# The first recurrence's columns taken out of the mixer, by seven products for eight, and the recurrence run beside the delta rule

## The chip, the core and the metric

The kernel runs on one core of a Trainium2 chip. The metric is device time in microseconds, the median of several runs. The engines are TensorE (PE; its weight loads are PEld), VectorE (DVE), ScalarE (ACT), GpSimd (POOL) and SyncE (SP), which here only starts DMAs.

## The reference, cut to what matters

One layer of a decoder: a feed-forward block (FFN), a mixer, a second FFN, a final norm, on 512 tokens of 1024 channels in float32.

```
h = x + 1/2 * SwiGLU_1(RMSNorm(x))
h = h + HybridMixer(RMSNorm(h))
h = h + 1/2 * SwiGLU_2(RMSNorm(h))
y = RMSNorm_final(h)
...
proj = (u @ w_in)
(hq, hf, hi, hg, gq, gk, gv, ga, gb, gz, gate_h, gate_g) = split(proj)
```

The mixer has two branches. The first recurrence (HGRN2, 8 heads) uses hq, hf, hi, hg: a forget gate from hf, a query silu(hq), values hi, an output gate silu(hg); its state is carried over chunks, its output normed and gated. The second (gated delta rule, 16 value heads, 8 query/key heads) uses gq, gk, gv after a short causal convolution, decays from ga and gb, an output gate silu(gz), and in each chunk the inverse of a unit lower triangular matrix. Each branch is projected to 1024 channels, the two are merged by sigmoid(gate_h) and sigmoid(gate_g), and one more projection follows.

## The kernel before, in words

Every operand of a large product is split into a high and a low half (`fp32r`), and three products (high by high, low by high, high by low; `mm3`, lines 188 to 191) stand for one float32 product. A "column" is 128 output channels for all 512 tokens: 8 slices of the 1024 input channels, three products each, so 24 products of 512 columns. Weights are read as `raw` tiles of 128 x 512; ScalarE casts the high half, VectorE subtracts for the low half. In some units the low half is made otherwise: ScalarE writes the negated high half, and a DMA started by GpSimd adds the weight from memory to it ("fold", lines 329 to 334).

**The FFNs** (`ffn`, line 448) run as a `stream` (line 282): a list of units, each one weight tile with its products. Before unit t runs, its halves must be there; `ahead` prepares up to some eight units in advance, in two lanes of three buffers. `posts` are what is done behind a unit, `hooks` what is done ahead of it. The first three pairs of columns (in the second FFN) are plain, 48 products of 512 columns a pair, while the norm is measured (`stats`, line 230) and the normalised operands are made (`operands`, line 426). The others are made by `fast` (line 354): a pair of columns as a two by two block product in Winograd's form, seven products for eight, 7 x 4 x 3 = 84 products of 256 columns, with sums of weights (`comb`) and of results (`sums`, lines 380 to 387) on VectorE.

**The mixer** (line 688) is ordered by a planner, `Desk` (line 64): each piece of work is a generator that asks for engines with estimated costs, buffers and events; the planner takes at each step the piece of lowest rank that is ready on an engine, and what it emits is the order of the instructions. SyncE's transfers are planned so too. `DENSE` (line 34) lists the columns in order: F and Q are hf and hq, B is hi and hg in natural layout (tokens on the partitions), D the decays, k, q, v, z the delta rule's, y the first branch's projection; the 16 gate columns t are taken when nothing else may start. `choose` (line 1679) says what each needs, `loader` (line 1696) starts the weight loads, `maker` (line 1728) splits them, `product` (line 1762) issues the products. The mixer's operands `uh`, `ul` are the input times its gain, but not times the norm: `norm` (line 1828) finds the norm, and each result is multiplied by it afterwards, on VectorE (`rbc`, in `h_q`, `h_f`, `conv`, `tgate`, `zgate`) or by a scalar (`rcol`, `h_v`, `gate`).

`h_head` (line 902) is one head of the first recurrence: products `pd` of queries and keys (line 917, four of 192 columns, in plain float32, two records each in the trace), seven levels of masked products `pl` (lines 974 and 980), mask copies (`copy_predicated`, line 938, four for each of the levels 2 to 16), then the chunks. Its eight heads stand, in `DENSE`, beside F, Q, B; most of the delta rule (`g_e`, `g_n`, `g_b`, `g_w`, `g_inv`, `g_rec`) comes behind them, when their buffers are passed on (`claim`, `more`). The triangular inverse of the delta rule runs on GpSimd. The heads' outputs stay in SBUF, split, as operands of y. `operand` (line 1526) reads the delta heads' outputs back for the last projection.

FFN and mixer each stand in a `tc.manual_schedule` block: inside of one, each engine's instructions keep the order in which they are written.

## Time and profile before

| | |
|---|---|
| median of three runs | 1606.91 us (1606.55 to 1606.93) |
| profiled execution, span | 1604.7 us |
| mean granted TensorE clock | 0.997 |
| instructions | 29242 |
| DMA | 204.91 MB, mean 128 GB/s |

The span reaches from the first to the last instruction of one profiled execution; the median of the runs is 2.2 us longer, with what lies around it. In the profile's rows a group stands by line, engine, operation and tiles, with its count, its busy time (overlaps counted once) and the mean duration of one, then the idle time ahead of it and what ended that. A duration of a product is longer than its place in the pipeline: products overlap. The table by stretches gives for each engine the busy time and, in brackets, the instructions. In the row of DMA issues the last number is the median time from issue to landing.

By time: the first FFN runs to about 358 us, the mixer to about 1245, the second FFN to the end; the masked products of the first recurrence run from 393 to 604, the delta rule to about 1110, the last two projections the rest.

### The profile page before, as it was taken

The numbers are of one execution on the slowest core, as the hardware profiler recorded it, in microseconds if no ns is written. First come the engines' busy times: TensorE is split into PE (matmuls) and PEld (weight loads), VectorE is DVE, ScalarE is ACT, GpSimd is POOL, SyncE is SP. The second block draws the span as 40 slices with busy tenths as digits, with TensorE's granted clock in tenths as the row PEclk, the third lists the DMA queues.
The fourth block names the chain that finished last, engine by engine and source line by source line (L and its number), as shares of the span: only waits on it lengthen the run. The fifth ranks groups of instructions, "written<-read, shape, count | busy, mean of one in ns | idle before, by whom it ended". The sixth has DMA issues, their size and how long they took to land.

```text
span 1604.7 us, 29242 instructions
## 1 busy us (share of the span) xinstructions
PE 1593.7 (99%) x10672; PEld 1386.3 (86%) x10672; DVE 1145.7 (71%) x2259; ACT 831.0 (52%) x1872; POOL 408.8 (25%) x725
## 2 busy tenths in 40 slices
PE   9999999999999999999999999999999999999997
PEld 8999998888888888888888888888888899999887
DVE  6888785447787778668788888765545788878433
ACT  5766674332434345456665665554324666667222
POOL 0211212001221221156545556600001121121001
PEclk9999999999999999999999999999999999999998
DMA  5766863332312322443242334445543586686333
GB/s 187 168 162 156 181 160 103 113 117 86 106 47 68 86 92 87 137 135 104 93 125 80 119 107 129 134 136 186 164 142 128 140 183 158 154 187 146 92 91 117
DMA packets 121824, 204.91 MB, mean 128 GB/s; under 512 B 21184, under 2 KB 27072, under 8 KB 121680
## 3 DMA queue, kind: packets, MB, share of 16 engines
q1 hardware_dynamic: 104688, 172.40, 34.3%
q0 software_dynamic: 14400, 26.22, 10.2%
q10 hardware_dynamic: 2592, 4.42, 1.0%
q8 instruction: 84, 1.38, 0.4%
q14 instruction: 60, 0.49, 0.1%
HBM read 188.02 MB, written 14.97 MB: 126 GB/s over the span
## 4 chain that ended last, share of the span: by engine, by line
PE 91%; DMA 3%; issue 3%; DVE 2%; ACT 0%; POOL 0%; POOLq 0%; SPq 0%; DVEq 0%; ACTq 0%
PE pmm L189 19%; PE pmm L191 19%; PE pmm L190 19%; PE px L191 6%; PE px L190 6%; PE px L189 6%; DMA wlo<-w1a 2%; PE pnat L189 2%; PE pnat L191 2%; PE pnat L190 2%; PE pgq L1189 1%; PE pw L1387 1%; PE pog L1403 1%; PE pl L974 1%; PE pd L917 1%
## 5 line engine op out<-in xcount | busy, mean ns | idle before, releaser
L189 PE MATMUL pmm<-uh,whi 128*128 128x512 f32 x879 | 361.3, 411 | 0.0
L191 PE MATMUL pmm<-uh,wlo 128*128 128x512 f32 x879 | 343.0, 390 | 0.0
L190 PE MATMUL pmm<-ul,whi 128*128 128x512 f32 x879 | 341.9, 389 | 0.0
L191 PE MATMUL px<-xs,wlo 128*128 128x256 f32 x1008 | 285.7, 283 | 1.3 <-DMA wlo<-w1a 0.7
L190 PE MATMUL px<-xs,whi 128*128 128x256 f32 x1008 | 285.2, 283 | 0.0
L189 PE MATMUL px<-xs,whi 128*128 128x256 f32 x1008 | 285.2, 283 | 0.0
L1754 ACT CAST whi<-raw 128x512 fp32r<-128x512 f32 x226 | 140.2, 621 | 242.7 <-PE pmm L190 195.2
L1756 DVE TENSOR_TENSOR wlo<-raw,whi 128x512 fp32r<-128x512 f32 x226 | 158.3, 702 | 118.2 <-ACT whi L1754 116.2
L191 PEld LDWEIGHTS pmm<-uh,wlo 128*128 128x128 f32 x879 | 165.0, 188 | 36.1 <-DVE wlo L607 0.2
L191 PEld LDWEIGHTS px<-xs,wlo 128*128 128x128 f32 x1008 | 193.5, 192 | 2.1 <-DMA wlo<-w1a 1.1
L189 PEld LDWEIGHTS px<-xs,whi 128*128 128x128 f32 x1008 | 193.5, 192 | 0.1
L190 PEld LDWEIGHTS px<-xs,whi 128*128 128x128 f32 x1008 | 193.5, 192 | 0.1
L189 PEld LDWEIGHTS pmm<-uh,whi 128*128 128x128 f32 x879 | 165.5, 188 | 30.4
L190 PEld LDWEIGHTS pmm<-ul,whi 128*128 128x128 f32 x879 | 165.7, 189 | 29.5 <-DVE ul L216 0.2
L329 ACT CAST whi<-sw 128x512 fp32r<-128x512 f32 x144 | 87.6, 613 | 92.8 <-DVE sw L366 72.6
L308 DVE TENSOR_TENSOR wlo<-raw,whi 128x512 fp32r<-128x512 f32 x100 | 77.7, 788 | 76.7 <-ACT whi L329 76.3
L329 ACT CAST whi<-raw 128x512 fp32r<-128x512 f32 x104 | 61.2, 592 | 125.6 <-PE pmm L190 92.8
L227 POOL TENSOR_TENSOR acc<-acc,sqt 128x512 f32<-128x512 f32 x18 | 23.4, 1302 | 319.8 <-ACT sqt L225 319.8
L308 DVE TENSOR_TENSOR wlo<-sw,whi 128x512 fp32r<-128x512 f32 x144 | 98.0, 681 | 0.0
L329 ACT CAST whi<-rw 128x512 fp32r<-128x512 f32 (+1 forms) x130 | 79.6, 613 | 26.6 <-PE px L190 13.4
L190 PE MATMUL pmm<-xs,whi 128*128 128x512 f32 (+1 forms) x238 | 89.7, 377 | 0.1
L189 PE MATMUL pmm<-xs,whi 128*128 128x512 f32 (+1 forms) x238 | 89.8, 377 | 0.0
(476 smaller groups left out, 3223.5 us busy)
## 6 DMA issues: line engine op xcount, KB each, us to landing
raw<-wt SPq DMA_DIRECT2D x160, 256.0 KB
rw<-w1b SPq DMA_DIRECT2D x80, 256.0 KB
rw<-w1a SPq DMA_DIRECT2D x74, 256.0 KB
wlo<-w1b POOLq DMA_DIRECT2D x53, 256.0 KB, 4.8
wlo<-w1a POOLq DMA_DIRECT2D x47, 256.0 KB, 5.0
raw<-w2b SPq DMA_DIRECT2D x41, 256.0 KB
raw<-w2a SPq DMA_DIRECT2D x36, 256.0 KB
raw<-wn SPq DMA_DIRECT2D x32, 256.0 KB
```

What stands on the lines that cost most here:

```text
L189: pe.matmul(pt, ah, bh, start=first, stop=False)
L190: pe.matmul(pt, ah, bl, start=False, stop=False)
L191: pe.matmul(pt, al, bh, start=False, stop=last)
L227: add.tensor_tensor(acc, acc, s, op=ALU.add)
L308: dve.tensor_tensor(lo, x, hi.bitcast(F32), op=ALU.subtract)
L329: act.copy(hi, x)
L917: pe.matmul(pd[c // 2][:, (c % 2) * 192:(c % 2) * 192 + 192], ke[:, c * P:(c + 1) * P], qq[:, c], start=True, stop=True)
L974: pe.matmul(pl_[s0:s0 + 32, c * 16:(c + 1) * 16], ke[:, c * P + s0:c * P + s0 + 32], qv[:, c, r, :, 1], start=True, stop=True)
L1189: pe.matmul(pq[:, (c % 2) * 256:(c % 2) * 256 + 256], kq[:, c, 0], kq[:, c].rearrange("p a b -> p (a b)"), start=True, stop=True)
L1387: pe.matmul(pw[:, hd2[i]], ut[:, 4 * i + c], xs[i], start=True, stop=True)
L1754: act.copy(hi, raw)
L1756: dve.tensor_tensor(lo, raw, hi.bitcast(F32), op=ALU.subtract)
```

## The change

A new stage, `projections`, stands between the first FFN and the mixer, in a `manual_schedule` block of its own, with two streams one behind the other.

- The first (pool `fp`): the eight columns of F and Q each, in pairs. Three pairs are plain (24 products of 512 columns a column) while the norm is measured; five go through `fast`, generalised by `outs`. Results go to memory (`qd`, `fd`), normed, Q through silu. `operands` gets a late form that leaves the normalised input, split, in `uh`, `ul`; four DMAs of GpSimd move half of it there. `decays`, before a piece of the planner's work, is done here at fixed units.
- The second (pool `bp`, opened after `fp` closes): `natural`, twice, each half of the columns of values and gates in natural layout as a block product with seven products for eight: 28 units of two times three products of 512 columns. The first product's four units and the third's four are folded. Results go to memory (`vd`, `gd`, silu on the gates). The first column of k follows in the same stream; its result is handed to the mixer in PSUM.

The stream's end now also runs posts that lie behind the last unit. In the mixer the columns F, Q, B, D are gone from `DENSE`, k0 too; the delta rule's come first, y last. Nothing is multiplied by the norm any more: `conv` and `tgate` read PSUM through ScalarE, `zgate` through ScalarE and VectorE. The heads read Q, F, values and gates back (`h_q`, `h_f`, `h_v`; Q into runs of 32 floats) and run at rank 2.5; each pair uses eight buffers `op`, reused. `pd` is made by sixteen products of 32 rows and 48 columns a head, and the masks up to 16 work on a compact tile `ac`, one copy a level in place of four, spread by four copies of ScalarE at the end. The heads' outputs go to memory (`hod`); `h_out` reads them back into `uh`, `ul` when all columns but y are done ("inputs"). Buffers of the delta rule are handed on by `give`, `allot`, `back`, `retire`. The gates' results all go through memory.

```diff
 DENSE = (
-    "F0 Q0 F1 Q1 B0 F2 Q2 F3 Q3 B1 D0 F4 Q4 F5 Q5 B2 F6 Q6 F7 Q7 B3 "
-    "k0 q0 k1 q1 y0 y1 y2 y3 v0 v1 y4 y5 y6 y7 k2 q2 v2 v3 z0 z1 k3 q3 v4 v5 z2 z3 k4 q4 v6 v7 z4 z5 "
-    "k5 q5 v8 v9 z6 z7 k6 q6 v10 v11 z8 z9 k7 q7 v12 v13 z10 z11 v14 v15 z12 z13 z14 z15 "
+    "q0 v0 v1 k1 q1 z0 z1 v2 v3 k2 q2 z2 z3 v4 v5 k3 q3 z4 z5 v6 v7 k4 "
+    "q4 z6 z7 v8 v9 k5 q5 z8 z9 v10 v11 k6 q6 z10 z11 v12 v13 k7 q7 z12 z13 v14 v15 z14 z15 "
+    "y0 y1 y2 y3 y4 y5 y6 y7 "
...
+RINGS = {False: RB, True: RW, "near": 8, "far": 5}
+AHEAD = tuple((k, i) for i in range(8) for k in "FQ")
+SLOW = 3
+HR = 2.5
...
+        for t in sorted(t for t in posts if t >= len(units)):
+            for f in posts[t]:
+                f()
...
+    def natural(p, xo, bp, at, posts):
...
+        units = []
+        for i in range(4):
+            units.append(Unit([a11[i], a21[i]], raw(a11[i]), prod(0, i, "mm"), drop=(a11[i],), fold=a11[i].src))
+        for i in range(4):
+            units.append(Unit([a22[i]], of("s2", i), prod(2, i, "aa"), comb=lambda i=i: sums(i)))
+        for i in range(4):
+            units.append(Unit([a12[i]], raw(a12[i]), prod(3, i, "bb"), drop=(a12[i],), fold=a12[i].src,
+                              comb=lambda i=i: comb("s4", i, a12[i], "s2", ALU.subtract)))
+        for n, o, lanes in (("s1", 1, "de"), ("s3", 4, "mm"), ("s4", 5, "aa")):
+            units += [Unit([], of(n, i), prod(o, i, lanes)) for i in range(4)]
+        for i in range(4):
+            units.append(Unit([], raw(a22[i]), prod(6, i, "bb"), drop=(a22[i],)))
+        return units
+
+    def projections(c0, ahead, weights, to, follow):
+
+        with tc.tile_pool(name="xp", bufs=1) as xp, \
+                tc.manual_schedule(engines={x.engine for x in (pe, act, dve, pool, sp)}):
+            xs = xp.tile([P, 24, T], F32R, name="xs")
...
+            with tc.tile_pool(name="fp", bufs=1) as fp:
...
+                for i in range(2 * SLOW):
+                    x, held = plain(weights(ahead[i]), KD, ux, lane if i < 2 else mm, fold=i > 3, roomy=lambda k: i % 2)
+                    units += x
...
+                    def two(v, i=i, o=o):
+                        act.activation(o[0][:, second], v["uc"][:, second], **shape(ahead[i]))
+                        sp.dma_start(to(ahead[i]), o[0])
+
+                    def three(v, i=i, o=o):
+                        act.activation(o[1][:, first], v["uc"][:, first], **shape(ahead[i + 1]))
+                        act.activation(o[1][:, second], v["vb"], **shape(ahead[i + 1]))
+                        sp.dma_start(to(ahead[i + 1]), o[1])
+                    units += fast([weights(x) for x in ahead[i:i + 2]], xo, fp, len(units), posts, (one, two, three), False)
...
+                stream(units, fp, 3, hooks, posts)
+            with tc.tile_pool(name="bp", bufs=1) as bp:
+                units, posts = [], {}
+                for p in range(2):
+                    units += natural(p, xo, bp, len(units), posts)
+                x, held = plain(weights(follow), KD, ux, lane, roomy=lambda k: "near")
+                units += x
+                stream(units, bp, 3, {}, posts)
+            return held["pt"]
...
-        for c in range(NT):
-            pe.matmul(pd[c // 2][:, (c % 2) * 192:(c % 2) * 192 + 192], ke[:, c * P:(c + 1) * P], qq[:, c],
-                      start=True, stop=True)
+        for c in range(NT):
+            for r in range(4):
+                s0 = 32 * r
+                pe.matmul(pd[s0:s0 + 32, c * 48:(c + 1) * 48], ke[:, c * P + s0:c * P + s0 + 32], qq[:, 4 * c + r],
+                          start=True, stop=True)
...
+    def h_out(k):
+
+        yield "on", ("oh", k), "inputs"
+        yield "get", "ta", 1
+        yield S
+        og = ta("og")
+        sp.dma_start(og, hod[k])
+        yield "lag", LAG["back"]
+        yield *A(512), 1
+        act.copy(uh[:, k], og)
+        yield *V(512), 1
+        dve.tensor_tensor(ul[:, k], og, uh[:, k].bitcast(F32), op=ALU.subtract)
...
     def conv(k, i, pt, out, n, lane="mm"):
-        dve.tensor_tensor(ci[:, 3:], pt, rbc, op=ALU.mult)
+        act.copy(ci[:, 3:], pt)
...
+    D.start((3, 8, -1), conv(("k", 0), 8, e["opened"], lambda: st[0]["kq"][:, :, 0], NT, "a"))
     D.start((3, -1), loader())
     D.start((9,), product())
     for i in range(8):
-        D.start((2, i), h_head(i))
+        D.start((HR, i), h_q(i))
+        D.start((HR, i), h_f(i))
+        D.start((HR, i), h_head(i))
+        D.start((7, i), h_out(i))
     for i in range(4):
-        D.start((2, i), h_pair(i))
+        D.start((HR, i), h_v(i))
```

More of the change, by code (lines that the diff above doesn't have):

```diff
@@ L509, in ffn, with silu, close @@
             for p in range(slow, KF):
-                units += fast(w1, p, xo, fp, len(units), posts, gate)
+                first, second = slice(0, 256), slice(256, 512)
+                def silu(n):
+                    return lambda v: act.activation(v[n][:, second], v[n][:, second], AF.Silu)
+                def close(v, p=p):
+                    gate(p, (v["ua"][:, second], v["uc"][:, second]), (v["uc"][:, first], v["vb"]))
+                units += fast([w1[ORDER[p], n] for n in range(2)], xo, fp, len(units), posts,
+                              (silu("ua"), silu("uc"), close), p >= 15 or p < 7)
             end = len(units)
@@ new lines, in give, with allot, back @@
+    def give(name, *items):
+        for x in items:
+            if (name, 7) in D.at:
+                retire(name, x)
+            else:
+                free[name].append(x)
+                D.put("p" + name)
+    def allot(name):
+        for u in range(8):
+            yield "get", "p" + name, 1
+            st[u][name] = free[name].pop(0)
+            D.fire((name, u))
+        for x in free[name]:
+            retire(name, x)
+    def back(u, *names):
+        for n in names:
+            give(n, st[u][n])
@@ L1117, in g_e @@
     def g_e(u, st):
[L1119 to L1120 removed]
+        yield "on", ("at", u), *([("E", u - 1)] if u else [])
         for i in range(2):
@@ L1658, in more @@
-        pool.memset(G["ut2"], 0.0)
-        D.fire(("ut", 2))
+        pool.memset(ut, 0.0)
+        new("ut", ut)
         e_ = ex(7, P, 4, 256)
-        for i, n in enumerate(("x", "we", "w")):
-            G[n].append(e_[:, i])
-        G["tp"].append(e_[:, 3].rearrange("p (a b) -> p a b", a=8))
-        D.fire("more")
+        new("rw", tuple(e_[:, i] for i in range(3)))
     todo = [(w[0], int(w[1:])) for w in DENSE.split()]
-    gates = [("t", i) for i in range(16)]
+    gates = [("t", i) for i in range(16) if i not in ahead]
@@ L1693, in choose @@
                 return x
-        return gates.pop(0) if len(gates) > (KEEP if todo else 0) else None
+        return gates.pop(0) if len(gates) > (KEEP if any(x[0] != "y" for x in todo) else 0) else None
     def loader():
```

913 lines of the change are left out of this document (422 added, 491 removed).

## The prediction

> **What bounds the kernel now.** The page comes first: busy times, then the slices, then the chain.
>
> ```profile
> span 1604.7 us, 29242 instructions
> PE 1593.7 (99%) x10672; PEld 1386.3 (86%) x10672; DVE 1145.7 (71%) x2259; ACT 831.0 (52%) x1872; POOL 408.8 (25%) x725
> PE   9999999999999999999999999999999999999997
> PEclk9999999999999999999999999999999999999998
> PE 91%; DMA 3%; issue 3%; DVE 2%; ACT 0%; POOL 0%; POOLq 0%; SPq 0%; DVEq 0%; ACTq 0%
> ```
>
> TensorE is busy in 1593.7 of 1604.7 us, in every slice but the last, at the full granted clock, and 91% of the chain that ended last is TensorE. So a microsecond of products removed is a microsecond gained, and a microsecond in which TensorE finds nothing ready, anywhere, is one lost. The change has to be added up in these two kinds.
>
> The table by stretches gives the price of a product where products run without a break, and the load of the other engines.
>
> ```profile
> core 0: us, PE busy (x) PEld busy (x) DVE busy (x) ACT busy (x) POOL busy (x), PEclk, DMA share, GB/s
> 1364.00:1404.10 40.10, 40.10 (x336) 40.10 (x336) 33.79 (x61) 25.05 (x50) 7.76 (x9) 1.00 0.68 154
> 1484.30:1524.50 40.20, 40.20 (x179) 33.28 (x178) 16.29 (x23) 10.99 (x20) 2.59 (x2) 1.00 0.32 92
> 361.00:682.00 321.00, 321.00 (x2674) 265.69 (x2673) 245.75 (x608) 133.91 (x324) 66.17 (x93) 1.00 0.30 89
> 682.00:1083.00 401.00, 401.00 (x2626) 332.77 (x2625) 319.90 (x701) 245.59 (x714) 213.79 (x490) 1.00 0.37 116
> 842.50:882.60 40.10, 40.10 (x283) 33.30 (x282) 35.67 (x84) 23.72 (x76) 22.66 (x55) 1.00 0.25 80
> ```
>
> First row, the seven-for-eight stage of the second FFN: 336 products of 256 columns in 40.10 us, 0.1193 us each. Second row, its plain products of 512 columns: 40.20 / 179 = 0.2246 us. The third row is roughly the first recurrence, the fourth the delta rule: VectorE is at 77% and 80%, and at 89% in the fullest stretch (last row) with TensorE still never idle.
>
> **The change, part by part: what goes.** Sixteen columns of F and Q are 16 x 24 = 384 products of 512 columns, 86.2 us. After: six plain columns (144 products, 32.3 us) and five pairs by seven products (5 x 84 = 420 of 256 columns, 50.1 us), 82.4 in all: **-3.8**. The values and gates in natural layout are
>
> ```profile
> L189 PE MATMUL pnat<-whi,uh 128*128 128x512 f32 x72 | 29.9, 415 | 0.0
> L189 PE MATMUL pnat<-wx,uh 128*128 128x512 f32 x56 | 22.6, 404 | 0.0
> L917 PE MATMUL pd<-qq,ke 128*128 128x192 f32 x64 | 11.5, 326 | 0.0
> L980 PE MATMUL pl<-qp,ke 128*32 128x32 f32 x128 | 2.8, 197 | 0.0
> L974 PE MATMUL pl<-qp,ke 128*32 128x16 f32 x1024 | 11.8, 185 | 0.0
> ```
>
> 128 products of each of three kinds, 384, 86.2 us; after, 2 x 7 x 4 x 2 x 3 = 336, 75.5 us: **-10.8**. The first score of each head (pd) now costs 64 records, 11.5 us; it becomes sixteen products of 32 rows and 48 columns a head, 256 records. Bounds: at the 11.5 ns of the 16-column products (11.8 / 1024) 2.9 us, at 1.5 times the 22 ns of the 32-column ones (2.8 / 128) 8.4. The second is nearer in shape: **-3**, ends -8.6 and 0. The Trainium skill (TensorE: Matmul & The Clock Gate, "Wait — 56ns, not 53.3ns?") states that starts of matmuls never follow each other closer than about 25 ns; by it the 256 take 6.4 us and this term is an estimated -5. The trace disagrees with that floor: 11.5 ns each in the last row.
>
> What remains of TensorE's work (delta rule, levels, transposes, all other columns) keeps its count, and interruptions of long products by short ones move with the short ones. Sum of what goes: **-17.6**.
>
> **What comes: the seam between the two new streams.** The FFN's weights reach the mixer early, since one hand-ordered block's instructions may overtake another's:
>
> ```profile
> 353.30 0.93 SPq L1712 DMA_DIRECT2D raw<-wt  x2
> 356.90 0.33 SPq L558 DMA_DIRECT2D hd<-h  x1
> 1244.13 0.69 DVE L1901 SCALAR_TENSOR_TENSOR h<-pmm,hr 128x512 f32<-128x512 f32 x1 [1.48 <-PE pmm L191]
> 1244.90 0.80 SPq L301 DMA_DIRECT2D rw<-w1b  x2
> 1247.68 0.62 ACT L329 CAST whi<-rw 128x512 fp32r<-128x512 f32 x1 [1.57 <-DMA rw<-w1b]
> ```
>
> The mixer's weight load at 353.30 goes ahead of the FFN's last spill at 356.90. But the second FFN's first load into a buffer of its own pool waits for the mixer's last instruction (1244.13 + 0.69) and starts at 1244.90; its data is used at 1247.68, 2.8 us later. In the change, both new streams stand in one block, so nothing overtakes, and the second's buffers lie where the first's were. The second's first four units also have their low half made by an accumulating DMA. So TensorE waits through a chain, from rows of the FFN:
>
> ```profile
> L385 DVE TENSOR_TENSOR uc<-px,uu 128x512 f32<-128x512 f32 x16 | 10.9, 681 | 0.0
> L407 ACT ACTIVATE uc<-uc 128x256 f32<-128x256 f32 x16 | 6.7, 418 | 4.8 <-DVE uc L385 4.8
> L329 ACT CAST whi<-rw 128x512 fp32r<-128x512 f32 x49 | 30.4, 620 | 7.9 <-PE px L190 6.4 <-DMA rw<-w1b 1.5
> L333 ACT ACTIVATE wlo<-whi 128x512 fp32r<-128x512 f32 x41 | 25.9, 632 | 1.3
> wlo<-w1b POOLq DMA_DIRECT2D x53, 256.0 KB, 4.8
> L588 PE MATMUL pwarm<-ones 128*128 128x128 f32 x22 | 4.8, 415 | 1.1 <-DVE mhalf L165 1.1
> L243 PE MATMUL pbc<-sq,rcol 128*128 128x128 f32 x16 | 2.1, 275 | 0.0
> ```
>
> Last sum 0.7; three activations 1.3; the store of the last column, which stands ahead of the loads on SyncE and holds the pool, 0.3 + 2.8 (no row has a store's landing; the load's is taken); the third load, 0.9 after the first, 2.8; cast and negation for two units (the second is prepared first) 2.5; accumulating DMA 4.8. With 0.5 for hand-overs, 16.6. Then the clock: the page's last slice shows it falling after short idle, and at the start 22 records of 128 columns take 4.8 us where 16 take 2.1 (2.9 for 22) later: 1.9 lost on each restart. **+18.5**; without the wait for the store and one unit's casts 14, with the twelve queued loads slowing the accumulation (4.8 doubled) 23.
>
> **The seam into the mixer.** SyncE's order in the mixer puts its rank first: the heads' Q, F, values and gates (six transfers, 2 MB; rank 2.5) ahead of the weights (rank 3). They go to the new pool, which waits for the old one's last store: sums 1.4, activation 0.7, store 3.1, then six issues of 0.4 and a load of 2.8, 10.4 after the last natural product; if 2 MB pass first at the 154 GB/s of the FFN row above, 13 us instead of 2.4, so 21. I take 13; cast and low half 1.3; less the one plain column kept to cover this, 24 x 0.2246 = 5.4; with 1.9 for the clock, **+11**, ends 0 (nothing held) and 19. The Trainium skill (DMA: Bandwidth & Descriptors, "Specifications") states that transfers under 512 B fall to read-modify-write; Q goes in by runs of 128 B, so by it the estimate would lean to the upper end. No row here shows it.
>
> **Smaller terms.** The y columns now wait until every other column is done, since their operands take the place of the normalised input:
>
> ```profile
> L1541 ACT CAST uh<-og 128x512 fp32r<-128x512 f32 x5 | 3.0, 617 | 0.0
> L1543 DVE TENSOR_TENSOR ul<-og,uh 128x512 fp32r<-128x512 f32 x5 | 3.3, 684 | 0.0
> ```
>
> At least 0.6 + 0.7 after the last such product, with the load 4.5, in an order laid out for later data 8: **+3**. In the fast stage VectorE carries the FFN's 33.79 of 40.10 and some 9 us of decays and operands over 50 us, near its fill: **+1** (0 to 5). In the mixer it loses the multiplications by the norm, three quarters of the mask copies and 64 weight halves, and does the rest, below 565.7 us (245.75 + 319.90), beside some 540 of products: about 81% by my count, under the 89% above; scalar work rises, hidden under its 61%: **+2** (0 to 10).
>
> At nothing I cost the added transfers: F, Q, values and gates go out by 32 stores of 256 KB and come back by 24 loads, the heads' outputs out and back by 16, some 21 MB in all. They lie beside products on queues that the rows above show 30% to 37% busy; if that cover were gone, 21 MB at the 116 GB/s of the fourth row would be 180 us, so even a tenth of it unhidden would outweigh everything else, and the six of them ahead of the mixer's first weights are that tenth's likeliest place, priced above. Behind a held load on SyncE stand all later loads and stores of its block, and TensorE waits for the first of them; elsewhere six prepared weight halves of buffer (three pairs a lane) cover it. The decays, moved into the fast stage, keep their products, and their table changes and VectorE work stand in that stage's +1.
>
> Sum: -17.6 + 18.5 + 11 + 3 + 1 + 2 = +17.9. 1604.7 + 17.9 = 1622.6; the median of the runs lies 2.2 above the span, so **1625**. With every term at its low end (-23.2 + 14 + 0 + 1.3) it would be 1599, with every term at its high end (-14.6 + 23 + 19 + 8 + 5 + 10) 1657; the ends do not fall together, and the forecast's own range is 1609 to 1643.
>
> **Rivals.**
> - *Seams covered.* If SyncE and ScalarE prepare the next stream while TensorE is still on the old one, as at 353.30, both seams cost nothing and the sum is -17.6 + 3 + 2: 1594 (1587 to 1600), faster. It decides where a stream's first weights are ready before the old stream's last product. For: no seam in the trace shows idle. Against: those are seams between blocks, and their first loads need no new pool.
> - *One seam.* If only the first one stalls, or the second does with half the first, the sum is near 0 to +7: 1605 to 1613.
> - *The end of the delta rule uncovered.* The gate columns, now used up as fill, no longer stand behind its last heads; eight y columns (43 us) do. If its last chain lags more than that, TensorE waits, perhaps 20 us on top: 1645. Against: the fourth row's POOL at 53% leaves slack.
> - *Not what it says*: if the recurrence still runs mostly ahead of the delta rule, only placement differs and no term changes.
>
> **Chances.** Forecast 0.56, covered 0.27, one seam 0.11, uncovered end 0.06. Only covered is clearly faster, and the one-seam case splits over all three. A measurement tells 0.2%, about 3 us, from no change. Faster 0.29, same 0.06, slower 0.65. The range takes in most of the covered case and of the forecast: 1590 to 1643; the forecast's own is 1609 to 1643.
>
> **What would show it.** Of after: idle of TensorE of over 10 us ahead of the first natural products, ended by an accumulating DMA; a second gap at the mixer's first columns, ended by a weight half; granted clock under 1.00 in both slices; 336 products of natural layout; pd with 256 records. If these gaps are absent, my reading of the order is wrong and the covered case holds; if pd or the fast stage costs more, the removal was mis-sized; idle among the last heads speaks for the uncovered end.

## The result, and the profile after

The changed kernel takes 1672.93 us (median of 4 runs, 1670.91 to 1674.61) where the kernel before takes 1606.92 (1606.55 to 1607.59): 1.0414 times as long, 95% interval 1.0401 to 1.0427. Forecast were 1625 us and a range of 1590 to 1643. The sign was the forecast one; the loss, 66 us, is more than three times the 18 that the sum gave.

The page of the profile after, to be read beside that of before: span, busy times, TensorE and its granted clock by slices, and the chain.

```profile
span 1671.7 us, 30224 instructions
...
PE 1603.4 (96%) x10996; PEld 1389.5 (83%) x10996; DVE 1145.7 (69%) x2168; ACT 910.8 (54%) x2025; POOL 433.6 (26%) x761
...
PE   9999999999959799999999999999999999999997
...
PEclk9999999999979999999999999999999999999999
...
PE 78%; DMA 8%; issue 7%; DVE 3%; ACT 1%; POOL 1%; SPq 0%; POOLq 0%; ACTq 0%; DVEq 0%
```

Two of forty slices fall to 5 and 7; elsewhere the tenths are too coarse to show anything. In the chain TensorE fell from 91% to 78%, and DMA and issue rose from 3% each to 8% and 7%. VectorE is busy for the same 1145.7 us as before.

The table by stretches of the changed kernel (columns as in the prediction: busy time and count of PE, PEld, DVE, ACT and POOL, granted clock, DMA share, GB/s) finds the places. The stretches are: the end of the plain F and Q columns, the fast stage, the seam between the streams, a stretch across the seam's end, the natural stage with its column k0, and the seam into the mixer.

```profile
362.00:395.00 33.00, 29.30 (x126) 24.03 (x125) 21.80 (x30) 16.69 (x26) 6.33 (x7) 0.95 0.59 166
395.00:460.90 65.90, 61.11 (x462) 58.76 (x460) 50.31 (x81) 46.47 (x83) 10.99 (x13) 0.95 0.65 168
460.90:480.00 19.10, 0.80 (x1) 0.29 (x1) 5.12 (x8) 6.86 (x13) 3.48 (x4) 0.62 0.81 235
465.60:486.10 20.50, 6.83 (x15) 5.07 (x16) 10.37 (x17) 7.14 (x12) 3.48 (x4) 0.50 0.98 286
480.00:575.30 95.30, 88.10 (x359) 70.04 (x359) 61.72 (x100) 46.41 (x78) 11.80 (x17) 0.95 0.53 141
575.30:586.30 11.00, 1.32 (x5) 0.71 (x4) 4.27 (x11) 2.94 (x6) 1.79 (x3) 0.64 1.01 285
```

None of these stretches has the full clock, not even those that the prediction thought covered. The view of TensorE's waits (total, times, longest, in us) gives each its cause; of the kernel before, the same view from 361 to 1244 us is empty.

```profile
PE pxn L197 <- DMA wlo<-wn: 14.6, 6, 7.4
PE pxn L196 <- ACT whi L336: 10.9, 1, 10.9
PE ptk L1284 <- DVE h L1255: 5.6, 1, 5.6
PE pmm L196 <- ACT whi L1841: 4.1, 1, 4.1
PE pbc L250 <- POOL rcol L259: 3.7, 1, 3.7
PE pn L593 <- issue: 3.5, 1, 3.5
PE pmm L196 <- ACT uh L1595: 3.0, 2, 1.5
PE pks L1508 <- DVE sm L1314: 2.1, 1, 2.1
```

The first row has six waits: 7.4 us end the first seam, five more, 7.2 us together, lie inside the natural stage. Rows 3 and 4 are the seam into the mixer, rows 5 and 6 the norm's spread and the decays' transposes, row 7 the last heads of the delta rule.

**The account.** Each product is given the start-to-start interval that its like has in an undisturbed stretch (226 ns for 512 columns, 120 for 256, 151 and 15 for the two forms of pd, and so on); the sum is TensorE's work. Of what the intervals are longer, those over 0.9 us are counted as waits, those in periods of half granted clock as half clock, and the rest as small delays. From the end of the first FFN to the start of the second:

```
                            total   work   waits  half clock  small
before  361 to 1244         883.0  838.8     0.0      0.0     44.2
after   362 to  395          33.1   27.2     3.9      1.6      0.3
        395 to  460.5        65.5   57.0     4.9      2.5      1.1
        460.5 to 480         19.5    0.3    19.1      0.0      0.0
        480 to  575          95.0   80.9     8.0      4.5      1.7
        575 to  586.4        11.8    0.9    10.2      0.8      0.0
        586.4 to 1311       724.2  652.2    14.6     10.2     47.2
after, sum                  949.1  818.5    60.6     19.6     50.4
after less before           +66.1  -20.3   +60.6    +19.6     +6.2
```

The work fell by 20.3 us, as it should; 60.6 us of waits and 19.6 of half clock came in its place. Some 35 us of it lie at the two seams (29.3 of waits, 6 of half clock), the rest in stages that the prediction took to be covered or nearly so.

### The profile page after: what moved, and what is told of

Same layout as the page of the kernel before. It is cut to its first block, busy times and chain, and to the rows that moved or that the text cites. A ratio compares the mean times of both kernels' runs of the same rounds, so it can differ in the third digit from the quotient of the medians.

```text
span 1671.7 us, 30224 instructions
## 1 busy us (share of the span) xinstructions
PE 1603.4 (96%) x10996; PEld 1389.5 (83%) x10996; DVE 1145.7 (69%) x2168; ACT 910.8 (54%) x2025; POOL 433.6 (26%) x761
## 2 busy tenths in 40 slices
DMA packets 156324, 236.32 MB, mean 141 GB/s; under 512 B 39424, under 2 KB 51328, under 8 KB 156176
## 4 chain that ended last, share of the span: by engine, by line
PE 78%; DMA 8%; issue 7%; DVE 3%; ACT 1%; POOL 1%; SPq 0%; POOLq 0%; ACTq 0%; DVEq 0%
PE pmm L196 17%; PE pmm L197 16%; PE pmm L198 16%; PE px L198 5%; PE px L196 5%; PE px L197 5%; DMA wlo<-w1a 2%; DMA wlo<-w1b 2%; DMA wlo<-wn 2%; PE pxn L197 1%; PE pxn L198 1%; PE pxn L196 1%; PE pgq L1328 1%; PE pw L1521 1%; PE pog L1537 1%
## 5 line engine op out<-in xcount | busy, mean ns | idle before, releaser
L196 PE MATMUL pmm<-uh,whi 128*128 128x512 f32 (+1 forms) x847 | 354.2, 418 | 7.2 <-ACT whi L1841 4.1
L198 PE MATMUL pmm<-uh,wlo 128*128 128x512 f32 (+1 forms) x847 | 335.2, 396 | 0.0
L197 PE MATMUL pmm<-ul,whi 128*128 128x512 f32 (+1 forms) x847 | 334.1, 394 | 0.2 <-DVE ul L1597 0.2
L198 PE MATMUL px<-xs,wlo 128*128 128x256 f32 x1128 | 320.6, 284 | 0.3 <-DMA wlo<-w1b 0.2
L196 PE MATMUL px<-xs,whi 128*128 128x256 f32 x1128 | 320.6, 284 | 0.0
L197 PE MATMUL px<-xs,whi 128*128 128x256 f32 x1128 | 320.2, 284 | 0.0
L196 PEld LDWEIGHTS px<-xs,whi 128*128 128x128 f32 x1128 | 217.6, 193 | 0.5 <-issue 0.2
L197 PEld LDWEIGHTS px<-xs,whi 128*128 128x128 f32 x1128 | 217.5, 193 | 0.1
L1843 DVE TENSOR_TENSOR wlo<-raw,whi 128x512 fp32r<-128x512 f32 x174 | 123.2, 711 | 119.6 <-ACT whi L1841 111.8
L1841 ACT CAST whi<-raw 128x512 fp32r<-128x512 f32 x174 | 107.7, 620 | 161.5 <-PE pmm L197 140.9
L336 ACT CAST whi<-raw 128x512 fp32r<-128x512 f32 x110 | 64.8, 593 | 136.5 <-PE pmm L197 94.4
L315 DVE TENSOR_TENSOR wlo<-raw,whi 128x512 fp32r<-128x512 f32 x104 | 80.2, 784 | 82.7 <-ACT whi L336 82.6
L336 ACT CAST whi<-rw 128x512 fp32r<-128x512 f32 (+1 forms) x151 | 92.4, 614 | 28.6 <-PE px L197 13.8
L196 PE MATMUL pmm<-xs,whi 128*128 128x512 f32 (+1 forms) x238 | 90.0, 378 | 0.0
L198 PE MATMUL pmm<-xs,wlo 128*128 128x512 f32 (+1 forms) x238 | 89.8, 377 | 0.0
```

The lines of the kernel that those rows point to most:

```text
L196: pe.matmul(pt, ah, bh, start=first, stop=False)
L197: pe.matmul(pt, ah, bl, start=False, stop=False)
L198: pe.matmul(pt, al, bh, start=False, stop=last)
L315: dve.tensor_tensor(lo, x, hi.bitcast(F32), op=ALU.subtract)
L336: act.copy(hi, x)
L1841: act.copy(hi, raw)
```

## The experiments

Three theories are tested. **A**: the loss is a sum of waits at fixed places, each with half clock behind it, and each can be taken away alone. **B**: the new stages are bound by VectorE or by what moves, so that a wait taken away comes back. **C**: the first recurrence beside the delta rule is what costs. Times are medians of 4 runs; the kernel before took 1605.8 to 1606.8 us beside each of them, and each ratio to it has an interval of about 0.0015 to either side, so that less than 3 us between two experiments says little.

**1. Low halves by VectorE.**

```diff
-units.append(Unit([a11[i], a21[i]], raw(a11[i]), prod(0, i, "mm"), drop=(a11[i],), fold=a11[i].src))
+units.append(Unit([a11[i], a21[i]], raw(a11[i]), prod(0, i, "mm"), drop=(a11[i],)))
```

and the same for a12.

> All sixteen low halves of the natural stage that an accumulating DMA made are made by VectorE instead (0.7 us each, 11 us more on VectorE, whose share of that stage is 62 of 95 us). Theory A (the loss is the sum of TensorE's stalls at fixed places, each with half clock behind it): the last 7.4 us of the first seam become about 1, the other waits for these DMAs (7.2 us in five) go, some 4 us of half clock behind them too: 15 to 19 us less than the changed kernel, 1654 to 1658. Rival B (the new stages are bound by what they move, and a stall that is taken away comes back at the next load): less than 6 us gained, 1667 or more, with the waits moved to the loaded slabs or to VectorE's sums.

Measured: 1664.53 us, 8.4 less, between what A and B gave. Waits inside the natural stage fall from 8.0 us to none, as A said, and half clock there from 4.5 to 2.0. But the seam, where A expected 6 us less, grew from 19.1 to 21.3. VectorE's timeline of this run has the reason:

```profile
475.39 0.69 DVE L648 TENSOR_TENSOR s<-near,far 128x512 f32<-128x512 f32 x1 [13.51 <-DMA far<-wn]
...
480.59 0.69 DVE L648 TENSOR_TENSOR s<-near 128x512 f32<-128x512 f32 x1
481.19 2.49 DVE L315 TENSOR_TENSOR wlo<-near,whi 128x512 fp32r<-128x512 f32 x4
```

The first low halves stand behind nine sums of slabs, the first of which waits for a load into the new pool. So taking the accumulating DMA away does not shorten the seam: the first 10.9 us, up to the first cast, are the same in both runs, and behind them the sums that the order puts first take the place of the DMA.

**2. The second stream begun inside the first.** The slabs' rings take the place of the normalised input and the decays' room, in the pool that both streams share, and the second stream's first loads and halves are issued from hooks of the first:

```diff
-                rooms = {n: fp.tile([P, m, T], F32, ...
+                rooms = {n: xp.tile([P, m, T], F32, ...
...
+                hooks.setdefault(n - 9, []).append(lambda: fetch(6))
+                hooks.setdefault(n - 7, []).append(lambda: fetch(4))
+                for t in (n - 3, n - 2, n - 1):
+                    hooks.setdefault(t, []).append(prepare)
```

> The natural stage's first ten slabs are loaded, and its first four pairs of halves made, while TensorE is still on the last fast unit: the slabs take the place of the normalised input and the decays' room, which are free by then, in a pool that both streams share. The first four low halves are made by VectorE. Theory A: the seam of 19.1 us shrinks to 0 to 3 us, the 6 us of products at half clock behind it go too, and one wait of 2 us: 20 to 25 us less than the changed kernel, 1648 to 1653. Rival B: the natural stage then waits for its later slabs instead, under 10 us gained, 1663 or more.

Measured: 1664.76 us, 8.2 less, a third of what A gave. TensorE's waits from 450 to 570 us in this run:

```profile
PE pxn L197 <- DMA wlo<-wn: 9.3, 3, 5.2
PE px L198 <- DMA wlo<-wt: 2.8, 1, 2.8
PE pxn L197 <- DVE wlo L321: 1.3, 1, 1.3
PE pxn L196 <- DVE uc L405: 0.8, 1, 0.8
```

Its accumulating DMAs of the natural stage, with their median from issue to landing in us, and then those of the changed kernel:

```profile
wlo<-wn POOLq DMA_DIRECT2D x12, 256.0 KB, 7.7
```

```profile
wlo<-wn POOLq DMA_DIRECT2D x16, 256.0 KB, 6.6
wlo<-wt POOLq DMA_DIRECT2D x14, 256.0 KB, 4.2
```

The seam is gone: the one wait left ahead of the first natural product is 0.8 us, for the last sum. But the preloads run beside accumulating DMAs that are under way: 2.8 us are lost in the old stream, and the waits for these DMAs in the new one are 9.3 us where the changed kernel had 7.2 behind its seam, with landings at 7.7 us instead of 6.6 and some 3.5 us more of half clock. The gain is what B gave, but the waits are for the accumulating DMAs and not for later slabs, as B had it. The two repairs need each other: with VectorE's halves alone (experiment 1) the pool and the sums still block them, with the preload alone the accumulating DMAs hold the products. Run 7, which has both, has 1.1 and 1.7 us of waits left there.

**3. Norm and decays later.**

```diff
-                hooks[1], hooks[2] = [sums], [spread]
+                hooks[1], hooks[4] = [sums], [spread]
...
-                (25, heads),
+                (28, heads),
```

with the operands two units and the decays' later steps three units later.

> The spread of the norm is issued two units later, and the decays' transposes, sums and rows three units later; nothing else is changed. Theory A: the waits of 3.7 us (norm) and 3.5 us (decays) go with 3.4 and 6.8 us of half clock behind them: 8 to 12 us less, 1661 to 1665. Rival B (VectorE is the bound of that stage, and whatever TensorE does not wait for here it waits for later): under 3 us, 1670 or more.

Measured: 1672.46 us, no change that can be told. The two waits went, but from 395 to 480 us new ones stand in their place:

```profile
PE px L198 <- DVE wlo L315: 2.6, 1, 2.6
PE pg L597 <- ACT nat L627: 2.5, 1, 2.5
```

The operands are late now where the norm was late before, and half clock in the fast stage rose from 2.5 to 4.8 us. B again: the operands' work on VectorE has no slack at the start of this stage, so moving these steps alone does not help.

**4. Weights ahead of the heads' loads in the mixer**, and **5. the y operands tile by tile.**

```diff
-    D.start((3, -1), loader())
+    D.start((2.4, -1), loader())
```

> In the mixer the weights' loads go ahead of the heads' loads on SyncE for the whole stage (a rank of 2.4 in place of 3). Theory A: TensorE's wait of 4.1 us for the first weight half goes, with some half clock; the wait of 5.6 us for the first convolution stays: 3 to 6 us less, 1667 to 1670. Rival C (the loss in the mixer comes from the first recurrence finishing late beside the delta rule): the heads are loaded later, so the end of the delta rule waits longer: 1673 or more.

Measured: 1666.67 us, 6.3 less, as A gave. The wait for the first weight half is gone, that for the convolution stays (5.9 us), and waits in the rest of the mixer fell from 14.6 us to about 11: no sign of C. Experiment 5, on the changed kernel alone:

```diff
-        yield "on", ("oh", k), "inputs"
+        yield "on", ("oh", k), "late" if k < 3 else ("in", k)
...
+        yield "on", ("in", k)
         yield *A(512), 1
         act.copy(uh[:, k], og)
```

where ("in", k) is fired behind the last other column's product of tile k.

> The y columns' weights are loaded as soon as no other column is left to load, the first three operands are loaded beforehand, and each operand is written as soon as the last other column has used the K tile that it replaces, rather than after that whole column. Theory A (sum of stalls): two waits of 1.5 us for the operands and 3 us of half clock behind them go: 4 to 6 us less than the changed kernel, 1667 to 1669. If the handover is bound by the delta rule's end instead, nothing changes: 1672 or more.

Measured: 1667.72 us, 5.2 less: the expected size from another place. The two waits of 1.5 us are still there. They are not the handover's but those of the delta rule's last two heads, whose outputs become operands of the closing products. What went are three smaller waits from 1095 to 1125 us (4.0 us, and 2.9 of half clock): with y available earlier, TensorE has something to do between the steps of the last heads.

**6. Three columns behind the natural stage instead of one.**

```diff
-... ("k", 0))
+... (("k", 0), ("q", 0), ("t", 0)))
```

> Three plain columns (k0, q0 and one gate column) instead of one stand behind the natural stage, so that 16 us of products are under way while the mixer's pool waits, its first loads land and the first convolution runs; the mixer makes two columns less. Theory A: the gaps of 6.0 and 4.5 us go with 3 us of half clock behind them: 10 to 13 us less, 1660 to 1663. Rival C (the columns are missed as fill later, beside the two recurrences and at the delta rule's end): under 4 us, 1669 or more, with new gaps between 590 and 1190 us.

Measured: 1666.95 us, 6.0 less, half of what A gave and more than C gave. The seam's waits shrink from 10.2 to 2.5 us, but new ones come later in the mixer:

```profile
PE pmm L196 <- ACT ci L1242: 4.7, 2, 4.1
PE pl L1133 <- DVE fl L1146: 3.4, 1, 3.4
```

Both lie near 680 us, in the first convolutions and in a level of the first recurrence: some of the wait moved.

**7. Everything together.**

> Everything together: the natural stage's slabs loaded one by one in the last twenty units of the first stream and their first halves made there, all its low halves by VectorE, the norm one unit and the decays three to five units later, weights ahead of the heads' loads, three columns behind the natural stage, the y operands written tile by tile. Theory A: 24 us of the first seam with its half clock, 9 of the natural stage, 11 to 13 of the second seam, 4 of small gaps in the mixer, 5 of the handover and 4 of norm and decays: 55 to 60 us less, 1613 to 1618. Rival B (bound by VectorE and by what moves, so that a stall taken away comes back elsewhere): half of that or less, 1640 or more.

Measured: 1624.08 us, 48.9 less than the changed kernel, 1.0111 times the kernel before (1.0096 to 1.0126). Single repairs gave between 0.5 and 8.4 us; together they give more than the sum of the parts (1, 2, 3, 5 and the larger of 4 and 6, which both shorten the same seam, make 28.6; with both it is 34.6). It is less than A's 55 to 60 and far more than B's half. The page and the waits from 362 to 1262 us of this run:

```profile
PE 1590.6 (98%) x10996; PEld 1381.4 (85%) x10996; DVE 1154.5 (71%) x2184; ACT 900.9 (55%) x2009; POOL 421.1 (26%) x745
...
PE   9999999999999999899999999999999999999997
```

```profile
PE pmm L196 <- ACT ci L1272: 4.5, 2, 3.9
PE pmm L196 <- ACT uh L1628: 3.1, 2, 1.5
PE px L198 <- DVE wlo L321: 2.6, 2, 2.4
PE pl L1162 <- POOL fm L1409: 2.2, 1, 2.2
```

By the account: work 819.4 from 362 to 1262 us, waits 19.6, half clock 7.0, small delays 54.3. That is 41 us of waits and 12.6 of half clock less than in the changed kernel. Theory A holds for the bulk of the loss, 49 of 66 us. These 49 are shown to come from order, buffers and the way in which low halves are made, and not from the products, which are the same in number (10996) and in work.

**8 to 10. What is left, by its suspects.** All three start from run 7: 8 makes q0 in the mixer again and gives two of VectorE's subtractions to GpSimd, 9 sets the recurrence's rank to 1.5 (the weights' loads stay ahead of it), 10 puts the heads' loads first again.

```diff
-HR = 2.5
+HR = 1.5
```

> As the run with everything together, but k0 and one gate column stand behind the natural stage (q0 is made in the mixer again, so one convolution fewer falls on VectorE at the mixer's start), and two of the three subtractions for the fast stage's operands go from VectorE to GpSimd. Theory A: the stalls left near 650 us (2.3 and 4.2 us, 10.2 us at half clock) come from VectorE being full there, with no unit of idle between 639 and 658 us, so they go with the convolution, 6 to 9 us less, and the wait of 2.7 us at the fast stage's start shrinks: 1613 to 1617. If the stall there is the first recurrence's own chain through GpSimd, it stays: 1621 or more.

> As the run with everything together, but the first recurrence goes ahead of every other work of the mixer but the weights' loads (rank 1.5 in place of 2.5). Rival C (running beside the delta rule delays the recurrence's chain, level by level behind the inversions on GpSimd, and so costs what is left): the stalls near 650 us go, 1614 to 1618. Theory A: the delta rule's own start is then later, and its end, which TensorE waits for at 1140 us already, later too: 1622 to 1632.

> As the run with everything together, but the weights' loads stand behind the heads' loads again, as in the changed kernel. With three columns behind the natural stage the second seam is covered either way, so by theory A the order costs 0 to 2 us: 1624 to 1626. If the gain of the earlier run with weights first (6 us) came from the whole mixer and not from the seam, it is lost here: 1628 or more.

Measured: 1636.57, 1623.96 and 1630.15 us. Run 8 is 12.5 worse, and what theory A expected of it fails on both counts: a wait of 4.1 us for a convolution's copy stays near 644 us, new ones come at 1058 and 1150 us, and the fast stage waits more (7.2 us against 5.7 in the view from 395 to 460 us). The wait that stays is not one of the recurrence's own chain either. Run 9 changes nothing, with the same waits at 648 and 652 us; so C is not right in the form that the recurrence comes too late in the order. Run 10 loses 6.1 us though its second seam is covered: the gain of experiment 4 came from the whole mixer, not from the seam alone.

**11 to 13. Fewer columns by seven products.** Run 11 is run 9 with SLOW = 6 (twelve plain columns; the last operands and the preloads are moved to fit), run 12 adds CONVS = 4. In these two the decays' rows overwrite one slab of sums of the natural stage; no instruction's count or shape changes by that. Run 13 is run 11 mended, with earlier preloads.

> As the run with everything together and the recurrence first, but twelve columns of F and Q by eight plain products and two pairs by seven, in place of six and five (the last operands and the preloads stand closer to fit). Products: 3 pairs x 0.76 us more, +2.3 us. Theory A: the fast stage lost 8 to 12 us to waits, half clock and short delays in 65 us, more than its five pairs save (3.8 us); with two pairs, some 5 to 7 of these go: 1618 to 1622. If those losses come from the decays and the operands' work wherever it lies, the time is 1625 to 1628.

> As the run beside it with twelve plain columns, but at most four of the convolved columns under way at once in place of seven, so that less of VectorE's work piles up at the mixer's start. If VectorE's crowd near 650 us makes the stalls there (2.3 and 4.4 us and half clock behind), 4 to 8 us less than the run beside it: 1612 to 1617. If the recurrence's chain makes them, or the columns put off are missed by the delta rule, the same or up to 10 us more.

> As the run with twelve plain columns, mended: the slabs of the natural stage are loaded from the twelfth to the sixth unit before its start, its last operands are written two units earlier, and the decays' rows are done before the sums that shared their place (the two runs before wrote the rows over one slab of sums). The earlier run had no wait of over 0.9 us left in its fast stage, but 8.5 us and 10 us at half clock ahead of the natural stage. Theory A: those 8.5 and some 5 behind them go: 1612 to 1616. If the seam only moves to the next sums, 1622 or more.

Measured: 1627.79, 1645.07 and 1620.82 us. In run 11 the fast stage has no wait over 0.9 us left, as A said, but one came ahead of the natural stage, and the time is 3.8 us above run 9, where the other reading had it:

```profile
PE pxn L197 <- DVE wlo L321: 8.4, 2, 8.1
```

Run 13 cuts it to 4.4 us (three waits) and lies between its two expectations. The stretch of F and Q shows the trade, first in run 7, then in run 13:

```profile
362.00:457.90 95.90, 89.68 (x587) 81.28 (x586) 74.84 (x115) 65.58 (x112) 17.38 (x20) 0.98 0.76 215
```

```profile
362.00:451.50 89.50, 88.77 (x477) 75.91 (x476) 52.27 (x78) 61.00 (x97) 22.52 (x26) 1.00 0.89 231
```

Three pairs back to plain products cost 2.3 us of work and the stage is 6.4 us shorter, with VectorE at 58% instead of 78%. As built here, seven products for eight lose in this stage, where VectorE also builds the operands and the decays. That is not isolated, since the decays, operands and loads stand elsewhere in run 13 too; and half of the gain is given back in the waits ahead of the natural stage, so that run 13 is 3.1 us better than run 9, hardly more than the noise. Run 12 is 17.3 worse than run 11, more than any of its readings gave: holding convolutions back starves the delta rule's end, where waits of up to 4.2 us then stand from 1129 to 1165 us.

**14 to 16. The mixer around run 13.** Run 14 sets TA = 7, run 15 leaves the first recurrence out, run 16 moves four z columns to the front of the list.

> As the run beside it, with seven buffers in the mixer's ring of short-lived tiles in place of six. TensorE waited 4.2 us at 652 us for a PSUM bank that the convolution's copy (ACT ci) empties, and that copy for such a tile. If the ring is what holds it: 3 to 6 us less than the run beside it, 1608 to 1612. If VectorE's crowd holds it, no change (within 2 us).

> As the best run so far (1620.8 us), without the first recurrence: its scores, levels, states and norm are left out, and its keys are stored as the heads' outputs, so that loads, stores and all columns stay. Its products take 43 us of TensorE by their undisturbed intervals. If running beside the delta rule costs nothing (theory A), the time falls by those 43 and the two stalls at 647 and 650 us with half clock (8 us): 1567 to 1573. Rival C (the recurrence delays the delta rule and its own chain on GpSimd and VectorE, which costs most of the 14 us that are left over before): 60 us or more less, 1561 or less.

> As the best run so far, with four z columns moved ahead of the first v and k columns in the mixer's list, so that fewer convolutions stand on VectorE while the recurrence's first heads run. If VectorE's crowd makes the stalls at 647 and 650 us (6.8 us of waits, half clock behind them): 5 to 9 us less, 1612 to 1616. If the delta rule is what its end waits for, the later v and k columns cost there what is gained here: 1619 to 1630.

Measured: 1639.40, 1573.29 and 1625.06 us. Runs 14 and 16 are 18.6 and 4.2 worse than run 13. In run 14 the wait for the convolution's copy is gone, so the ring did hold it, but larger waits come at 1053 and 1147 us; run 16 spreads the waits. Run 14 fits neither of its readings, run 16 the second. Run 15 is 47.5 less, at the upper end of what A gave (1573) and on the far side of it from C. But it brings a wait of its own, and ScalarE, which makes the copy that TensorE waits for, stands idle just before it for a store of the heads' outputs, as its timeline shows:

```profile
PE pmm L196 <- ACT ci L1127: 14.5, 1, 14.5
```

```profile
604.03 0.72 ACT L1100 ACTIVATE oh<-hb,cs 128x512 f32<-128x512 f32 x1 [7.13 <-DMA hod<-oh]
```

In run 13 the copy (ci, of a convolution) for which TensorE waits 4.2 us stands instead behind the last step of an earlier convolution on VectorE, so the wait of 14.5 us belongs to run 15 alone: apparently, with no recurrence between them, the heads' outputs follow one another faster than they are stored. Without it run 15 would lie near 1559 us, an estimate from the 14.5 us, and that is in C's range. Its other waits in the mixer are 2.8 us, against 12.8 in run 13. So run 15 does not decide between A and C for what is left. What goes beside the 43 us of work is 13.6 us of small delays (34.8 in the mixer, 48.4 in run 13): short products between long ones. The kernel before has 44.2 us of these with the recurrence mostly ahead of the delta rule, so most of this price was paid in either place.

What stays open is why the mixer keeps some 11 us of waits, and whether the recurrence brings them by its order or by its load on the engines that both recurrences use: six changes of the mixer's order or its rings (runs 8, 9, 10, 12, 14 and 16) left them or made them larger, mostly in another place, and no run that keeps the recurrence took them away. No such version beats the kernel before; the nearest is run 13, at 1.0091 (1.0074 to 1.0108).

## Why the prediction was right in its sign and wrong in its size

The sum missed by 48 us: 20 in the mixer with its handover, 13 in the first stream (F and Q), 11 in the natural stage and 6 at the two seams, less 3 for products that were removed beyond the forecast. The sign was no luck: the two seams, which were foreseen, cost 35 us, more than the 20 that went. What failed is the step that took the other stages as covered, by the share of VectorE's time or by prepared halves.

- **What bounds the kernel.** Right. TensorE without idle before, so products removed and waits added are all that counts; the account above closes to 1 us of the spans' difference.
- **What goes, -17.6.** Measured -20.3. The natural layout is as forecast (336 products of 512 columns). The score products were mis-sized, within the stated ends: 9.7 us by start-to-start intervals before, 3.7 after (without one wait of 1.1), -6 instead of -3.

```profile
L1070 PE MATMUL pd<-hb 128*32 128x48 f32 x256 | 4.4, 209 | 0.0
```

  By the intervals that is 14 ns each; the step from 16 columns (11.5 ns) to 48 costs little. The Trainium skill's floor of about 25 ns (TensorE: Matmul & The Clock Gate, "Wait — 56ns, not 53.3ns?") would make 6.4 us of them and does not hold for these products of 32 rows.
- **First seam, +18.5.** Right, in place and cause: 19.1 us of waits and some 3 of half clock up to 486 us. Of the chain worked out beforehand, the cast came after 10.9 us (forecast about 10), and the accumulating DMA took 7.3 where 4.8 had been taken and 9.6 was the upper end:

```profile
471.57 0.90 POOL wlo L341
472.47 0.25 issue
472.74 7.28 DMA wlo<-wn
480.06 0.80 PE pxn L197
```

- **Second seam, +11.** Right in size: 10.2 of waits and 3 of half clock. The cause was half seen. The weight half is there (4.1), but ahead of it TensorE waits 5.6 us for the convolution of k0, the very column that was kept as cover: the planner's order puts its transposes before the next products. The convolution itself starts late, at 573.8 us, since VectorE waits 3.0 us for the old pool's last store.
- **Fast stage, +1 (0 to 5).** The step that failed first. The prediction counted VectorE's load and found it near its fill; it did not ask what stands at a fixed unit, and priced no wait for the plain columns ahead of the stage. The norm's spread and the decays' transposes stand at units 2 and 25 and were not ready: with a wait of 1.1 us for a low half, 8.8 us of waits, 4.1 of half clock, 1.4 of small delays, 14 us in all. Experiment 3 shows that the places alone are not the cause: with these two steps later, the operands behind them are late.
- **Natural stage, at nothing.** The second failed step: "elsewhere six prepared weight halves of buffer (three pairs a lane) cover it". They do not. The accumulating DMAs land after 6.6 us in the middle where 4.8 was taken, and TensorE waited for five more of them: 11 us with half clock (past 486 us) and small delays. Experiment 1 shows it, as these waits go with the DMAs. What moves in the whole kernel grew by 31.4 MB (204.91 to 236.32), where the prediction counted 21.
- **The mixer, +2 (0 to 10), and the handover, +3.** The third, and the largest: together 25 us measured (14.6 of waits, 7.8 of half clock past the seam, 3 of small delays). 7 us are the late y columns (4.0 and 2.9 from 1095 to 1125 us, gone in experiment 5), 6 the delta rule's last heads (3.4 and 2.8 from 1185 to 1200 us), which is the rival of the uncovered end, at a third of its price. The other 12 us are single waits from 660 to 825 us, the longest of 2.1, with half clock and short delays; their causes were not taken apart. VectorE, forecast at 81%, is busy for 70% of this stretch (511.55 of 735.70 us from 575.3 us on); its mean share says nothing of these waits, which are those of single chains.
- **Half clock.** Priced for two restarts at 1.9 us. Between 362 and 1311 us it was there eight times and cost 19.6 us, 2.5 each. A single wait of 2.1 us brought it, as the rows show, the first TensorE's wait, the second the stretch behind it:

```profile
740.73 0.67 PE L1508 MATMUL pks<-s,h 128*128 128x256 f32 x2 [2.14 <-DVE sm L1314]
```

```profile
742.10:745.50 3.40, 3.40 (x23) 2.71 (x11) 2.12 (x7) 0.40 (x1) 2.08 (x5) 0.50 0.25 94
```

- **Rivals.** "Covered" was wrong for this code; the first seam was covered only by the rewrite of runs 2 and 7. "One seam" is excluded, since both stall. "Not what it says" is excluded: the recurrence runs from 597 to 865 us, beside the delta rule.

## What to carry to other kernels

A kernel whose bound engine is never idle has no average slack: a new stage must be read for every step that stands at a fixed place in the order, and for each the chain that must be done by then, not for the share of the engine that does it. A stream of work that ends in a pool and begins in another costs the whole latency from the last result to the first operand, plus half clock; start the next stream's loads and first operands inside the old one, in memory that is free by then. Repairs of such a seam can hang together: here the preload alone gave a third of what was expected of it, so try them together before judging the change.

## What the hardware showed that was not expected

The granted clock falls to half for periods that are multiples of about 3.4 us (3.4, 6.8, 13.7 and 20.5 us in the changed kernel). A period begins some 2 to 5 us after the first wait does and outlasts the last one by 3 to 6 us, so that short waits are paid mostly after they are over. The Trainium skill (TensorE: Matmul & The Clock Gate, "HAM oscillation — how this bites in real kernels") gives the rule that gaps of over some 3.4 us are to be avoided; by the rows above one of 2.1 us was enough, and twice in the mixer, at 1104 and 1189 us, two of 1.4 to 1.6 us with under 2 us between them were, so here the measurement decides. Not every wait has it. Of these two in the natural stage (TensorE's timeline of the changed kernel, the wait in brackets) the second has a period of 3.4 us behind it, from 527.1 us, the first none:

```profile
497.05 0.50 PE L197 MATMUL pxn<-wlo,xs 128*128 128x512 f32 x1 [1.62 <-DMA wlo<-wn]
...
526.85 0.61 PE L197 MATMUL pxn<-wlo,xs 128*128 128x512 f32 x1 [2.42 <-DMA wlo<-wn]
```

An accumulating DMA of 256 KB landed after 4.2 us in the middle in the first stream, 6.6 in the second, and 7.7 in that of experiment 2. In the second stream of the changed kernel its latency follows what else is moving. The four issued from 519 to 523 us landed after 8.6 us in the middle, the four from 534 to 540 us after 5.0; the last two numbers of the stretches in which they were under way are the share in which the DMA engines were busy, and what they moved:

```profile
519.00:532.70 13.70, 11.28 (x42) 8.57 (x40) 12.64 (x21) 7.12 (x13) 3.43 (x4) 0.88 1.03 276
534.20:546.40 12.20, 9.85 (x42) 7.51 (x42) 2.97 (x5) 6.45 (x12) 3.44 (x4) 1.00 0.59 95
```

So buffers that are sized by the 4.8 us of a quieter stage were too few here.
